# Twenty instead of sixteen seven-product pairs in the second MLP product of a hybrid decoder layer

## The chip, the cores and the metric

The kernel runs on one core of a Trainium2 chip. The metric is the time of one execution on the device in microseconds (us); less is better. The engines are named as the profile names them: PE (TensorE's matmuls) and PEld (its weight loads), DVE (VectorE), ACT (ScalarE), POOL (GpSimd) and SP (SyncE, which issues the weight loads from memory here).

## The reference

One decoder layer over 16 learned meta tokens and 256 input tokens of width 2048, in float32. Four mixers (S5, mLSTM, FoX, Pool) stand between two projections; then comes the MLP. Its last product, 256 tokens x 8192 by 8192 x 2048, is the stage that the change touches:

```python
D_MODEL = 2048
SEQ = 256
D_FF = 4 * D_MODEL
...
hn = rmsnorm(h, g_pre_ffn[l])
ff = jnp.square(jax.nn.relu(hn @ mlp_w1[l])) @ mlp_w2[l]
h = h + rmsnorm(ff, g_post_ffn[l])
```

## The kernel before

**Numbers.** Each float32 operand is split into a rounded part and the rest (high and low), and a product is three matmuls: high by high, high by low, low by high. ACT makes the high part by a cast (`wh`, line 155, and `ah`, line 201), DVE the low part by a subtraction (`wl`, line 156, and `al`, line 202). The order is fixed on each engine: DVE's subtraction waits for ACT's cast, and PE's matmuls wait for both.

**Stages.** All four projections of the layer run as one list of jobs (`stream`, line 133). A job is 1 MB of weights in two halves of 512 KB, each loaded by one transfer that SP issues (`load_job`, line 123). PE consumes half by half; the loop over halves splits weights `LOOK = 3` halves ahead into four buffers of each kind (`wsp`), and loads go three jobs ahead. The staging buffers are `wst` (8 tiles) and, apart from them, `wss` (2 tiles, one job).

**The second MLP product** (`fast_jobs`, line 286) is computed in two parts of 1024 output columns each. A part has 32 jobs, called pairs, since each covers two blocks of 128 of the 8192 inner elements. A letter in `KINDS` (line 53) says how a pair is computed:

- N, plain (`plain`, line 319): 2 inner blocks x 2 token blocks x 2 column blocks are 8 block products, three matmuls each (lines 310 to 312): 24 matmuls of 512 columns. Its weights come through `wst` and the splits at lines 155 and 156, its activations through `split_act` (line 196).
- S, seven products (`seven`, line 346): a Strassen-Winograd form with 7 block products, 21 matmuls, 9 in its first half and 12 in its second. It needs sums of weight blocks and of activation blocks ahead of its matmuls, and these are split as well. Its weights come through `wss`.

The work ahead of an S pair is a list of seven steps, taken in this order: `raw` (splits of three raw weight blocks, lines 348 and 349), `act_sums` (split of the raw activations, and four sums on POOL, lines 351 and 367), `sums1` (two differences on DVE, line 351), `act_split` (split of the activation sums), `split1` (split of two sums), `sums2` (two more differences) and `split2`. The split results stand in parts of the tile `xc`, which is free after the first MLP product. There is one copy of them, so the steps of an S pair can write a part of it only once the matmuls of the S pair before have read it; and the loads of an S pair can start only once the splits of the S pair before have read `wss`.

**The order around the change.** `stream` decides at which half i of the job list a step is recorded. `at` is the number of the S pair's first half. Steps of the first S pair begin 6 halves ahead of it, those of each later one 2 halves behind the first half of the S pair before, which is right after that pair; they are spread evenly over the halves up to 4 ahead of `at`:

```python
sums[0]["from"] = sums[0]["at"] - 6
...
left = max(1, s["at"] - 3 - i)
for _ in range(-(-len(s["steps"]) // left)):
    s["steps"].pop(0)(s["stage"])
```

Beneath, a scheduler of the tile framework turns the recorded order into one list for each engine. After the last S pair of a part its sums (in PSUM banks M1, M5, M6, M7) are combined on ACT and DVE (lines 406 to 413); the last pair (first part) or last two pairs (second part) are held and run output block by output block, and each block is then normalized, scaled and, at the end, written out.

Of the kernel before, what the change touches and what calls it, by code (L numbers as in the profile page):

```python
# [49 lines left out]
LOOK = 3  # L50
PACE = 2.0
LOOP = (2.5, 4.0, 3.0)
KINDS = ("NNNS" * 7 + "NNSN", "NNS" + "NNNS" * 6 + "NNSNN")


def build(tc, A, out):
# [10 lines left out]
class Body:  # L67
# [65 lines left out]
    def stream(self):  # L133
        nc = self.nc
        jobs = self.jobs
        sums = [j for j in jobs if "steps" in j]
        sums[0]["from"] = sums[0]["at"] - 6
        halves = [(j, h) for j in jobs for h in range(2)]
        split = {}

        def do_split(i):
            j, h = halves[i]
            if "steps" in j:
                return
            src = j["stage"][h]
            if j.get("early"):
                wh = self.sb(self.post, [P, 1024], f"wh{j['early']}{h}", F32R)
                wl = self.sb(self.post, [P, 1024], f"wl{j['early']}{h}", F32R)
            else:
                wh = self.sb(self.wsp, [P, 1024], "wh", F32R)  # L150
                wl = self.sb(self.wsp, [P, 1024], "wl", F32R)
            n = 512 if i == 0 else 1024
            for a in range(0, 1024, n):
                cs = slice(a, a + n)
                nc.scalar.copy(wh[:, cs], src[:, cs])  # L155
                nc.vector.tensor_tensor(out=wl[:, cs], in0=src[:, cs], in1=wh[:, cs].bitcast(F32), op=ALU.subtract)  # L156
            split[i] = (wh, wl)
            if j.get("pre"):
                j["pre"](h)

        done = 0
        early = [i for i, (j, h) in enumerate(halves) if j.get("early")]
        for i, (j, h) in enumerate(halves):
            self.load(i // 2 + 3)
            if i == early[0] - 2:
                self.load(early[-1] // 2 + 1)
            while done < i + LOOK + 1 and done < len(halves) and (done not in early or i >= early[0] - 2):
                with ExitStack() as es:
                    if early[-1] < done <= early[-1] + LOOK + 1:
                        for ins in self.after:  # L170
                            es.enter_context(self.tc.issue_after(ins))
                    do_split(done)
                done += 1
                if done - 1 in early:
                    while done in early:
                        do_split(done)
                        done += 1
                    break
            if sums and i >= sums[0]["from"]:
                s = sums[0]  # L180
                if "stage" not in s:
                    self.load_job(s, -1)
                left = max(1, s["at"] - 3 - i)
                for _ in range(-(-len(s["steps"]) // left)):
                    s["steps"].pop(0)(s["stage"])
                if not s["steps"]:
                    sums.pop(0)
                    if sums:
                        sums[0]["from"] = s["at"] + 2
            if i == 0:  # L190
                self.load_s5()
            self.pull(PACE + min(0.0, self.credit))
            wh, wl = split.pop(i, (None, None))
            j["mm"](h, wh, wl)
# [1134 lines left out]
    def ffn_jobs(self):  # L1329
# [82 lines left out]
        ta, tm = ["a0", "a1", "a2", "a3"], ["m0", "m1", "m2", "m3"]  # L1412
        jobs += self.fast_jobs(w2, NF, act2, 0, tm, ta, KINDS[0], 2, part_a, evac_a)
        jobs += self.fast_jobs(w2, NF, act2, 1024, ta, tm, KINDS[1], 4, part_b, evac_b)
        return jobs
# [26 lines left out]
```

## Time and profile before

| what | value |
|---|---|
| median of 3 runs | 1120.52 us (1120.06 to 1123.67) |
| the profiled execution, its own time | 1118.29 us |
| span of that execution | 1116.6 us |
| PE busy | 1092.6 us (98%), 6377 matmuls |
| DVE busy | 786.3 us (70%) |
| ACT busy | 600.6 us (54%) |
| POOL busy | 178.6 us (16%) |
| read from memory | 199.58 MB |

The profile lists, for one execution, each instruction of each engine with its start and duration. The duration of a matmul is modelled and overlaps the next one, so what a matmul takes is read from starts. In brackets behind a row stands the idle time of its engine in front of it, and what ended that. The span leaves out 1.7 us of the execution around it.

### The profile page before, as it was taken

How to read it: one execution, taken by the hardware profiler on the slowest of the kernel's cores; microseconds unless marked ns; L12 is line 12 of the kernel's file. 1: busy time of each engine (PE TensorE's matmuls, PEld its weight loads, DVE VectorE, ACT ScalarE, POOL GpSimd, SP SyncE). 2: the span in 40 equal slices, each digit the busy share in tenths (PEclk: the TensorE clock that was granted, in tenths of full speed). 3: DMA queues.
4: the chain of work that ended last, by engine and by line, in shares of the span. 5: the costliest groups of instructions: out<-in, count | busy, mean ns of one | idle time of the engine just before them, and what ended most of it. 6: DMA issues, size and time to landing. Idle time of an engine off the chain costs nothing.

```text
span 1116.6 us, 16901 instructions
## 1 busy us (share of the span) xinstructions
PE 1092.6 (98%) x6377; PEld 949.8 (85%) x6377; DVE 786.3 (70%) x1094; ACT 600.6 (54%) x919; POOL 178.6 (16%) x222
## 2 busy tenths in 40 slices
PE   8999999999999999999999999999999999999996
PEld 7899999888977878888888888888888888888885
DVE  6589997655555675555555555558788789997886
ACT  5576443356555566454445444546665555765562
POOL 7810320101342011100000000001121120421101
PEclk9899999999999999999999999999999999999998
DMA  8646555554446636666666666666546655666542
GB/s 253 194 128 191 152 151 152 159 152 127 133 154 230 233 126 218 189 188 189 188 186 188 188 186 188 187 189 227 197 172 205 223 176 187 229 194 230 197 151 76
DMA packets 94707, 203.35 MB, mean 182 GB/s; under 512 B 15877, under 2 KB 19073, under 8 KB 94369
## 3 DMA queue, kind: packets, MB, share of 16 engines
q1 hardware_dynamic: 93680, 201.46, 58.0%
q8 instruction: 50, 0.82, 0.3%
q10 hardware_dynamic: 848, 0.79, 0.2%
q14 instruction: 33, 0.26, 0.1%
q0 software_dynamic: 96, 0.02, 0.0%
HBM read 199.58 MB, written 2.11 MB: 181 GB/s over the span
## 4 chain that ended last, share of the span: by engine, by line
PE 92%; POOL 3%; DMA 2%; DVE 1%; ACT 1%; issue 1%; DVEq 0%; SPq 0%; POOLq 0%; ACTq 0%
PE m L1353 11%; PE a L1353 11%; PE a L223 6%; PE a L224 6%; PE a L225 6%; PE a L1354 6%; PE m L1354 6%; PE m L311 5%; PE m L312 5%; PE m L310 5%; PE a L311 5%; PE a L310 5%; PE a L312 5%; PE a L252 4%; PE m L252 3%; POOL row L734 1%
## 5 line engine op out<-in xcount | busy, mean ns | idle before, releaser
L156 DVE TENSOR_TENSOR wl<-wst,wh 128x1024 fp32r<-128x1024 f32 (+1 forms) x255 | 311.2, 1226 | 150.9 <-ACT wh L155 150.6
L155 ACT CAST wh<-wst 128x1024 fp32r<-128x1024 f32 (+1 forms) x255 | 265.7, 1045 | 216.6 <-PE m L1353 54.0
L1353 PE MATMUL m<-xc,wh 128*128 128x512 f32 x512 | 180.2, 394 | 0.1
L1353 PE MATMUL a<-xc,wh 128*128 128x512 f32 x512 | 179.5, 393 | 0.0
L223 PE MATMUL a<-xc,wh 128*128 128x272 f32 (+2 forms) x576 | 168.7, 295 | 0.4 <-ACT wh L155 0.4
L224 PE MATMUL a<-xc,wh 128*128 128x272 f32 (+2 forms) x576 | 167.6, 292 | 0.0
L225 PE MATMUL a<-xc,wl 128*128 128x272 f32 (+2 forms) x576 | 166.3, 291 | 0.0
L156 DVE TENSOR_TENSOR wl<-wss,wh 128x1024 fp32r<-128x1024 f32 x78 | 95.9, 1230 | 75.0 <-ACT wh L155 74.8
L1354 PE MATMUL a<-xc,wl 128*128 128x256 f32 x512 | 144.1, 282 | 0.0
L1354 PE MATMUL m<-xc,wl 128*128 128x256 f32 x512 | 144.1, 282 | 0.0
L155 ACT CAST wh<-wss 128x1024 fp32r<-128x1024 f32 x78 | 81.6, 1047 | 90.8 <-PE m L1353 29.4
L1353 PEld LDWEIGHTS m<-xc,wh 128*128 128x128 f32 x512 | 96.0, 187 | 22.3 <-DVE xc L1309 0.3
L1353 PEld LDWEIGHTS a<-xc,wh 128*128 128x128 f32 x512 | 95.9, 187 | 22.1
L223 PEld LDWEIGHTS a<-xc,wh 128*128 128x128 f32 x576 | 110.0, 192 | 4.5 <-issue 2.2
L224 PEld LDWEIGHTS a<-xc,wh 128*128 128x128 f32 x576 | 110.5, 192 | 1.0 <-issue 0.4
L225 PEld LDWEIGHTS a<-xc,wl 128*128 128x128 f32 x576 | 109.4, 191 | 0.8 <-issue 0.4
L351 POOL TENSOR_TENSOR sums<-h 128x128 f32<-128x128 f32 x12 | 20.5, 1712 | 498.3 <-DVE xc L349 468.3
L1354 PEld LDWEIGHTS a<-xc,wl 128*128 128x128 f32 x512 | 96.5, 188 | 0.1
L1354 PEld LDWEIGHTS m<-xc,wl 128*128 128x128 f32 x512 | 96.5, 189 | 0.0
L348 ACT CAST xc<-wss 128x512 fp32r<-128x512 f32 (+1 forms) x64 | 59.8, 941 | 36.4 <-DVE wss L351 28.5
L310 PE MATMUL m<-wh,ah 128*128 128x512 f32 x192 | 74.7, 389 | 0.0
L311 PE MATMUL m<-wl,ah 128*128 128x512 f32 x192 | 74.7, 389 | 0.0
(371 smaller groups left out, 1929.0 us busy)
## 6 DMA issues: line engine op xcount, KB each, us to landing
wst<-in_mlp_w SPq DMA_DIRECT2D x182, 512.0 KB, 4.2
wss<-in_mlp_w SPq DMA_DIRECT2D x74, 512.0 KB, 3.7
wst<-in_w_in SPq DMA_DIRECT2D x49, 512.0 KB, 3.9
wss<-in_w_in SPq DMA_DIRECT2D x22, 512.0 KB, 3.7
wst<-in_w_out SPq DMA_DIRECT2D x20, 512.0 KB, 3.6
wss<-in_w_out SPq DMA_DIRECT2D x12, 512.0 KB, 5.2
x<-in_x SPq DMA_DIRECT2D x8, 256.0 KB, 7.4
res<-in_x SPq DMA_DIRECT2D x1, 2048.0 KB
```

The source lines that it names most:

```text
L155: nc.scalar.copy(wh[:, cs], src[:, cs])
L156: nc.vector.tensor_tensor(out=wl[:, cs], in0=src[:, cs], in1=wh[:, cs].bitcast(F32), op=ALU.subtract)
L223: nc.tensor.matmul(acc[:, :nt], sh, xh(k, t0, nt), start=(k == 0), stop=False)
L224: nc.tensor.matmul(acc[:, :nt], sh, xl(k, t0, nt), start=False, stop=False)
L225: nc.tensor.matmul(acc[:, :nt], sl, xh(k, t0, nt), start=False, stop=(k == nk - 1))
L252: ins = nc.tensor.matmul(acc[tok, c], sp[k][a][:, tok * P:(tok + 1) * P], w2[b][:, c * 512:(c + 1) * 512], start=(k == 0 and (a, b) == (0, ...
L310: nc.tensor.matmul(b, ah, wh, start=first, stop=False)
L311: nc.tensor.matmul(b, ah, wl, start=False, stop=False)
L312: return nc.tensor.matmul(b, al, wh, start=False, stop=stop).ins
L348: nc.scalar.copy(wh, src)
L1353: nc.tensor.matmul(acc.rearrange("p (a b) -> p a b", a=2), wh[:, ws], XC[:, k, :, 0:S], start=(k == 0), stop=False)
L1354: nc.tensor.matmul(acc[:, 0:S], wl[:, ws], XC[:, k, 0, 0:S], start=False, stop=(k == NK - 1))
```

## The change

`KINDS` now has an S in every third place, ten in each part, with two N at the end: 20 S pairs and 44 N pairs instead of 16 and 48. With a period of three pairs (six halves), the steps are recorded closer together. The first S pair's begin 4 halves ahead of it instead of 6. Its loads are recorded one half before its first step. A later S pair's steps begin one half earlier than before, behind the first half of the S pair in front of it: one step there, and the other six spread up to the half that is 2 ahead of its own first.

```diff
@@ -50,7 +50,7 @@
 LOOK = 3
 PACE = 2.0
 LOOP = (2.5, 4.0, 3.0)
-KINDS = ("NNNS" * 7 + "NNSN", "NNS" + "NNNS" * 6 + "NNSNN")
+KINDS = ("NNS" * 10 + "NN", "NNS" * 10 + "NN")
 
 
 def build(tc, A, out):
@@ -134,7 +134,7 @@
         nc = self.nc
         jobs = self.jobs
         sums = [j for j in jobs if "steps" in j]
-        sums[0]["from"] = sums[0]["at"] - 6
+        sums[0]["from"] = sums[0]["at"] - 4
         halves = [(j, h) for j in jobs for h in range(2)]
         split = {}
 
@@ -176,17 +176,19 @@
                         do_split(done)
                         done += 1
                     break
-            if sums and i >= sums[0]["from"]:
+            if sums and i >= sums[0]["from"] - 1:
                 s = sums[0]
                 if "stage" not in s:
                     self.load_job(s, -1)
-                left = max(1, s["at"] - 3 - i)
-                for _ in range(-(-len(s["steps"]) // left)):
+
+                left = s["at"] - 1 - i
+                for _ in range(0 if i < s["from"] else 1 if i == s["from"] else -(-len(s["steps"]) // left)):
                     s["steps"].pop(0)(s["stage"])
                 if not s["steps"]:
+                    assert left >= 1
                     sums.pop(0)
                     if sums:
-                        sums[0]["from"] = s["at"] + 2
+                        sums[0]["from"] = s["at"] + 1
             if i == 0:
                 self.load_s5()
             self.pull(PACE + min(0.0, self.credit))
```

In the new program every line after 186 has a number 2 higher (156 stays, 202 is 204, 310 is 312, 349 is 351, 351 is 353). On TensorE's list 12 matmuls fewer stand; VectorE has 28 subtractions more.

On VectorE, in the middle of the first part, a period of the kernel before, from the last two splits of one S pair (line 349) to the first of the next (`wss` are its staging tiles; lines 156 and 202 belong to N pairs):

```order
L349 TENSOR_TENSOR xc_71<-wss_8547,xc_71 128x1024
L156 TENSOR_TENSOR wl_8579<-wst_8535,wh_8578 128x1024
L349 TENSOR_TENSOR xc_71<-wss_8548,xc_71 128x1024
L202 TENSOR_TENSOR al_8603<-h_4654,ah_8602 128x512
L156 TENSOR_TENSOR wl_8599<-wst_8536,wh_8598 128x1024
L156 TENSOR_TENSOR wl_8651<-wst_8634,wh_8650 128x1024
L202 TENSOR_TENSOR al_8675<-h_4654,ah_8674 128x512
L156 TENSOR_TENSOR wl_8671<-wst_8635,wh_8670 128x1024
L156 TENSOR_TENSOR wl_8688<-wst_8666,wh_8687 128x1024
L202 TENSOR_TENSOR al_8712<-h_4654,ah_8711 128x512
L156 TENSOR_TENSOR wl_8708<-wst_8667,wh_8707 128x1024
L349 TENSOR_TENSOR xc_71<-wss_8715,xc_71 128x512
```

The same stretch of the change:

```order
L351 TENSOR_TENSOR xc_71<-wss_8606,xc_71 128x1024
L156 TENSOR_TENSOR wl_8707<-wst_8686,wh_8706 128x1024
L351 TENSOR_TENSOR xc_71<-wss_8607,xc_71 128x1024
L204 TENSOR_TENSOR al_8731<-h_4654,ah_8730 128x512
L156 TENSOR_TENSOR wl_8727<-wst_8687,wh_8726 128x1024
L156 TENSOR_TENSOR wl_8748<-wst_8722,wh_8747 128x1024
L204 TENSOR_TENSOR al_8772<-h_4654,ah_8771 128x512
L156 TENSOR_TENSOR wl_8768<-wst_8723,wh_8767 128x1024
L351 TENSOR_TENSOR xc_71<-wss_8734,xc_71 128x512
```

Between the steps of two S pairs lie the splits of two N pairs (four of `wl`, two of `al`) where those of three lay; the steps themselves have the same order.

On SyncE, the loads of one period before:

```order
L131 DMA wss_8547<-in_mlp_w 128x1024
L131 DMA wst_8498<-in_mlp_w 128x1024
L131 DMA wss_8548<-in_mlp_w 128x1024
L131 DMA wst_8499<-in_mlp_w 128x1024
L131 DMA wst_8535<-in_mlp_w 128x1024
L131 DMA wst_8536<-in_mlp_w 128x1024
L131 DMA wst_8634<-in_mlp_w 128x1024
L131 DMA wst_8635<-in_mlp_w 128x1024
L131 DMA wss_8715<-in_mlp_w 128x1024
```

and of the change:

```order
L131 DMA wss_8478<-in_mlp_w 128x1024
L131 DMA wst_8558<-in_mlp_w 128x1024
L131 DMA wss_8479<-in_mlp_w 128x1024
L131 DMA wst_8559<-in_mlp_w 128x1024
L131 DMA wst_8594<-in_mlp_w 128x1024
L131 DMA wst_8595<-in_mlp_w 128x1024
L131 DMA wss_8606<-in_mlp_w 128x1024
```

Two loads of N pairs fewer stand between one S pair's loads and the next; one still stands between the two loads of an S pair.

## Rows read from the trace of the kernel before

**Rows 1.** The page's engine totals, and its chain of waits by engine.

```profile
PE 1092.6 (98%) x6377; PEld 949.8 (85%) x6377; DVE 786.3 (70%) x1094; ACT 600.6 (54%) x919; POOL 178.6 (16%) x222
...
PE 92%; POOL 3%; DMA 2%; DVE 1%; ACT 1%; issue 1%; DVEq 0%; SPq 0%; POOLq 0%; ACTq 0%
```

**Rows 2.** Busy time by windows: a steady stretch, and the joint of the parts.

```profile
core 0: us, PE busy (x) PEld busy (x) DVE busy (x) ACT busy (x) POOL busy (x), PEclk, DMA share, GB/s
840.00:860.00 20.00, 20.00 (x90) 16.57 (x89) 16.62 (x19) 12.51 (x15) 3.29 (x4) 1.00 0.57 196
940.00:960.00 20.00, 20.00 (x90) 16.57 (x89) 19.19 (x25) 13.93 (x22) 0.67 (x1) 1.00 0.67 215
```

**Rows 3.** Timeline of PE around an S pair (start, duration, what).

```profile
866.65 0.39 PE L310 MATMUL m<-wh,ah 128*128 128x512 f32 x1
866.88 0.39 PE L311 MATMUL m<-wl,ah 128*128 128x512 f32 x1
...
869.37 0.39 PE L310 MATMUL a<-xc,ahR 128*128 128x512 f32 x1
...
874.13 0.39 PE L310 MATMUL m<-wh,ah 128*128 128x512 f32 x1
```

**Rows 4.** Timeline of DVE through the steps of an S pair.

```profile
846.86 1.23 DVE L156 TENSOR_TENSOR wl<-wst,wh 128x1024 fp32r<-128x1024 f32 x1 [1.15 <-ACT wh L155]
848.92 0.69 DVE L202 TENSOR_TENSOR al<-h,ah 128x512 fp32r<-128x512 f32 x1 [0.84 <-ACT ah L201]
...
851.01 1.83 DVE L349 TENSOR_TENSOR xc<-wss,xc 128x512 fp32r<-128x512 f32 x2
852.76 0.68 DVE L351 TENSOR_TENSOR wss<-wss 128x512 f32<-128x512 f32 x1
...
854.56 1.82 DVE L351 TENSOR_TENSOR wss<-wss,wss 128x512 f32<-128x512 f32 x2
856.42 0.83 DVE L351 TENSOR_TENSOR wss<-wss 128x512 f32<-128x512 f32 x1
857.17 1.48 DVE L349 TENSOR_TENSOR xc<-wss,xc 128x1024 fp32r<-128x1024 f32 x1
858.58 1.21 DVE L156 TENSOR_TENSOR wl<-wst,wh 128x1024 fp32r<-128x1024 f32 x1
859.71 1.21 DVE L349 TENSOR_TENSOR xc<-wss,xc 128x1024 fp32r<-128x1024 f32 x1
860.85 0.68 DVE L202 TENSOR_TENSOR al<-h,ah 128x512 fp32r<-128x512 f32 x1
861.45 1.21 DVE L156 TENSOR_TENSOR wl<-wst,wh 128x1024 fp32r<-128x1024 f32 x1
```

**Rows 5.** Timeline of ACT: the cast that the split at 846.86 waits for.

```profile
845.77 1.05 ACT L155 CAST wh<-wst 128x1024 fp32r<-128x1024 f32 x1 [1.32 <-PE m L312]
```

**Rows 6.** Timelines of DVE and PE at the joint of the two parts.

```profile
951.09 1.22 DVE L156 TENSOR_TENSOR wl<-wst,wh 128x1024 fp32r<-128x1024 f32 x1
...
953.91 1.07 PE L311 MATMUL a<-wl,ah 128*128 128x512 f32 x4
```

**Rows 7.** Timeline of POOL: the first of its four sums of an S pair.

```profile
854.12 0.84 POOL L351 TENSOR_TENSOR sums<-h 128x128 f32<-128x128 f32 x1 [17.63 <-DVE xc L349]
```

**Rows 8.** Timelines of SP (the loads for the next S pair) and ACT (their second reader).

```profile
858.68 0.33 SPq L131 DMA_DIRECT2D wss<-in_mlp_w  x1
859.82 0.33 SPq L131 DMA_DIRECT2D wst<-in_mlp_w  x1
860.95 0.33 SPq L131 DMA_DIRECT2D wss<-in_mlp_w  x1
...
850.53 1.05 ACT L348 CAST xc<-wss 128x1024 fp32r<-128x1024 f32 x1 [0.18 <-PE m L312]
```

**Rows 9.** The page's DMA issues: count, KB each, median us to landing.

```profile
wss<-in_mlp_w SPq DMA_DIRECT2D x74, 512.0 KB, 3.7
...
wss<-in_w_out SPq DMA_DIRECT2D x12, 512.0 KB, 5.2
```

**Rows 10.** The chain that ended last: where it leaves PE.

```profile
1100.51 0.24 PE a L312
```

## Prediction

> **What bounds the kernel now.** I read the profile's engine totals and its chain of waits first. TensorE is busy for 98% of the span and carries 92% of the chain that ended last [rows 1]. So a change can gain by taking matmuls away, or lose by making TensorE wait. Next come the busy times in windows of the second MLP product. In a steady stretch TensorE has no idle time at a granted clock of 1.00 (the higher level, 2.4 GHz); VectorE is busy 16.62 of 20 us, ScalarE 12.51, GpSimd 3.29. At the joint of the product's two parts VectorE reaches 19.19, and TensorE is still full [rows 2]. So TensorE alone bounds this product, and VectorE is next in line.
>
> The rows of TensorE give the size of each kind of pair [rows 3]. The second half of a plain pair (N) starts at 866.65 and the seven-product pair (S) behind it at 869.37: 12 matmuls in 2.72 us, 0.2267 us each. The S pair ends where the next N begins, at 874.13: 21 matmuls in 4.76 us. A plain pair has 24, so it takes 5.44 us. The listed duration of 0.39 us is a modelled end; the starts, 0.2267 us apart, are what a matmul costs.
>
> **What VectorE does meanwhile** [rows 4]. Starts that follow each other without a wait give a cost of 1.13 us for a split of 1024 elements (858.58 to 859.71) and 0.60 us for one of 512 (860.85 to 861.45). An N pair asks two of the first and one of the second, 2.86 us. The steps of one S pair run from 851.01 to 860.85 with one weight split of an N pair among them: 9.84 - 1.13 = 8.71 us. A period NNNS is 3 x 5.44 + 4.76 = 21.08 us of TensorE and 3 x 2.86 + 8.71 = 17.29 us of VectorE; the other 3.79 us are waits such as the 1.15 us at 846.86 and the 0.84 us at 848.92. They end on ScalarE's casts, and the cast in front of the first of them waited 1.32 us for a matmul [rows 5]: TensorE had not yet let go of a buffer. VectorE idles because it is as far ahead as the buffers allow, so these waits are the cover, not a cost.
>
> How deep that cover is shows in one place: the split that starts at 861.45 ends at 862.66, and its first reader is the matmul at 866.88 [rows 3, 4]. Even right behind the steps of an S pair the data is 4.22 us early. At the joint it is least: a split ends at 952.31 and is read at 953.91, 1.60 us early [rows 6].
>
> **The change, part by part.** *Matmuls.* There were 16 S pairs, 8 in each part, and now there are 20. Each of the four more replaces 24 matmuls by 21, so 12 go: 12 x 0.2267 = 2.72 us. All lie on the path, since TensorE never waits in this product. The Trainium skill (page "TensorE: Matmul & The Clock Gate", section "Back-to-back issue gap") gives about 131 ns per matmul of 512 columns in a sustained stream; the rows show 226.7 ns, so the measurement decides; by the page the sum would be 1.6 us.
>
> *Steps of four more S pairs.* Each adds 8.71 us to VectorE and takes an N pair's 2.86 us away. Both parts now run in periods of NNS: 2 x 5.44 + 4.76 = 15.64 us of TensorE against 2 x 2.86 + 8.71 = 14.43 us of VectorE. The spare is 1.21 us a period where it was 3.79. It is thin but positive, so VectorE still regains its full lead before each block of steps, and the block, unchanged in content, still leaves about the 4.22 us that it leaves now. I cost it at 0. If the cover is gone, every us over 15.64 is paid in each of 20 periods. ScalarE stands at 12.51 of 20 us [rows 2], and a denser mix does not bring it near its limit: 0 as well.
>
> *GpSimd's sums.* They run directly behind the step that frees their buffer, after 17.63 us of waiting for VectorE [rows 7], so they are ready a whole period early; a period that is 5.44 us shorter leaves about 12 us. What they cost is VectorE's speed beside them: two operations from 854.56 to 856.42 instead of 1.20 us, one of 0.75 instead of 0.60, one of 1.41 instead of 1.13: 0.66 + 0.15 + 0.28 = 1.09 us, already inside the 8.71.
>
> *The loads of S pairs.* The staging buffers are freed by the last two splits of the steps; the second load is issued at 860.95 [rows 8] and lands 3.7 us later by the median [rows 9], at 864.65. Its first reader is ScalarE's cast, one period behind the one at 850.53 [rows 8], so at 871.61, 6.96 us later. With one N pair fewer, 5.44 us of that go: 1.5 us are left. That is 0 at the median, and the order in which SyncE issues the loads keeps two plain loads among and two behind these. With the slowest median landing on the page, 5.2 us [rows 9], it just fits.
>
> *Start and joint.* The first S pair is the third instead of the fourth. It has 5.44 us less, of which VectorE needed 2.86 for the N pair, so at worst 2.58 us are lost; I take 0, because in steady periods the block needs no more room than NNS gives, and 2.58 as the other bound. At the joint one more N pair now lies between the last S pair of the first part and the first of the second, so the tight spot gets easier. The end, from the last sums on, has the same instructions in the same order; it moves with TensorE.
>
> **Sum.** The profiled execution took 1118.29 us, 1116.6 of it the span. 1118.29 - 2.72 = 1115.57. The median of the runs shown is 1120.52, 2.23 above that execution, so the forecast is 1120.52 - 2.72 = **1117.8 us**, 0.24% below. About 0.3%, 3.4 us, is what a measurement of this kernel can tell from no change: this gain is real but below that.
>
> **The rivals.** *VectorE becomes the bound* (the other side). It decides once a block of steps costs over 8.71 + 1.21 = 9.92 us. The way there is GpSimd: were VectorE held for all of GpSimd's 3.29 us a block [rows 2] instead of 1.09, the block would be 10.91 us, the period 16.63, and 0.99 us x 20 periods would be lost: 1117.8 + 19.8 = 1137.6 us. For it speaks that the spare shrinks from 3.79 to 1.21 us. Against it speaks that VectorE completes operations in those us, at 0.75 to 0.93 instead of 0.60 [rows 4], and that the 19.19 of 20 us at the joint cost TensorE nothing. The Trainium skill (page "SBUF — State Buffer", section "Who interferes with whom") says that a VectorE instruction with two SBUF inputs and a GpSimd instruction that reads SBUF exclude each other, so that the second waits for the whole of the first; by that rule this rival would win, but the trace shows a slowing by about half. Chance 4%.
>
> *The S loads come late.* Landing later than 3.7 + 1.5 + 1.21 = 6.4 us stalls TensorE in each period; at 7 us it is 0.6 x 20 = 12 us: 1129.8. Nothing shown lands that late by the median; more bunched loads speak for it. Chance 4%.
>
> *A stall in one place only*, at the first S pair: up to 2.58 us back, 1120.4 us. Chance 8%.
>
> **How the numbers follow.** The forecast has 84%. That the change isn't there is no case: the order of TensorE's work has just 12 matmuls fewer. Runs of the same program spread from 1118.29 to 1123.67; both less 2.72 give the range, **1115.6 to 1121.0 us**, which also takes in the local stall. Within the forecast the step from 0.24% to 0.3% is 0.6 us, small against that spread, so I give three tenths of it to faster: 0.25. Slower by over 0.3% are the two rivals, 0.08. Within 0.3%: 0.67.
>
> **What would show it.** TensorE full in every window of this product, with starts 0.227 us apart; the matmul that now stands at 1100.51 on the chain [rows 10] at about 1097.8; VectorE near 18.5 of 20 us in steady windows (14.43 of 15.64), its waits for ScalarE mostly gone. Wrong would be: starts of TensorE over 0.3 us apart at the head of S pairs, each a period from the last, released by VectorE (first rival), or by ScalarE's cast behind a late load (second).

## The result, and the profile after

The changed kernel takes 1130.26 us (median of 6 runs, 1127.95 to 1130.98) beside 1119.28 us for the kernel before (6 runs, 1116.20 to 1123.67): a ratio of 1.0099, 95% interval 1.0083 to 1.0115. The forecast was 1117.8 us and a gain of 0.24%; it is a loss of 1%, and outside the range.

The page's engine totals and its chain of waits by engine:

```profile
PE 1095.4 (97%) x6365; PEld 947.2 (84%) x6365; DVE 804.4 (71%) x1122; ACT 603.4 (53%) x931; POOL 189.5 (17%) x238
...
PE 73%; DVE 10%; DMA 8%; issue 4%; POOL 3%; ACT 2%; SPq 0%; DVEq 0%; ACTq 0%; POOLq 0%
```

Twelve matmuls fewer (6365 instead of 6377), as worked out. But the chain that ended last, 92% TensorE in [rows 1], is now 73% TensorE, with 10% VectorE and 8% DMA: TensorE waits. Where it does is told by windows of the second MLP product (columns as in [rows 2]: busy us and instructions of each engine, TensorE's granted clock, DMA share, GB/s):

```profile
840.00:860.00 20.00, 20.00 (x90) 16.58 (x89) 17.60 (x20) 12.70 (x17) 3.30 (x4) 1.00 0.59 188
860.00:880.00 20.00, 19.55 (x87) 15.85 (x86) 16.70 (x20) 10.49 (x14) 3.30 (x4) 1.00 0.57 185
880.00:900.00 20.00, 19.39 (x85) 15.55 (x84) 16.23 (x19) 9.57 (x13) 3.30 (x4) 1.00 0.61 206
900.00:920.00 20.00, 19.14 (x83) 15.16 (x83) 16.58 (x19) 11.63 (x15) 3.29 (x4) 1.00 0.60 208
920.00:940.00 20.00, 18.93 (x82) 14.75 (x80) 17.27 (x22) 11.66 (x15) 4.43 (x6) 1.00 0.49 160
940.00:960.00 20.00, 17.42 (x62) 13.49 (x63) 20.00 (x26) 12.14 (x21) 2.22 (x3) 0.83 0.61 197
...
1020.00:1040.00 20.00, 20.00 (x90) 16.54 (x89) 17.60 (x20) 12.37 (x16) 3.30 (x4) 1.00 0.63 204
...
1080.00:1100.00 20.00, 19.49 (x86) 15.80 (x85) 17.04 (x21) 10.33 (x13) 3.29 (x4) 1.00 0.51 165
```

A full window holds 90 matmuls. The first part is full up to 860, then the windows are short of 3, 5, 7 and 8; the joint is short of 28; the second part starts full and is short again at its end. A shortage that sets in late is the mark of a lead that is eaten period by period. TensorE's first waits in this product, a period of 16.72 us apart, stand near the end of an S pair and are released by its last split:

```profile
876.61 0.50 PE L313 MATMUL a<-xc 128*128 128x512 f32 x1 [0.45 <-DVE xc L351]
...
893.33 0.50 PE L313 MATMUL a<-xc 128*128 128x512 f32 x1 [0.61 <-DVE xc L351]
```

So VectorE is late with that split, but not for its load: it is busy 16.2 to 17.3 us of 20 in the first part's short windows, below the 18.5 that the prediction expected of a full mix. (At the joint it is busy throughout, 20.00 us.) It waits. Its timeline over one period, and ScalarE's behind it:

```profile
872.80 1.48 DVE L351 TENSOR_TENSOR xc<-wss,xc 128x1024 fp32r<-128x1024 f32 x1
...
875.34 1.21 DVE L351 TENSOR_TENSOR xc<-wss,xc 128x1024 fp32r<-128x1024 f32 x1
...
881.09 0.68 DVE L351 TENSOR_TENSOR xc<-wss,xc 128x512 fp32r<-128x512 f32 x1
883.96 1.23 DVE L351 TENSOR_TENSOR xc<-wss,xc 128x1024 fp32r<-128x1024 f32 x1 [2.19 <-ACT xc L350]
...
889.52 1.48 DVE L351 TENSOR_TENSOR xc<-wss,xc 128x1024 fp32r<-128x1024 f32 x1
890.93 1.21 DVE L156 TENSOR_TENSOR wl<-wst,wh 128x1024 fp32r<-128x1024 f32 x1
892.06 1.21 DVE L351 TENSOR_TENSOR xc<-wss,xc 128x1024 fp32r<-128x1024 f32 x1
```

```profile
878.32 0.62 ACT L350 CAST xc<-wss 128x512 fp32r<-128x512 f32 x1 [0.25 <-DMA wss<-in_mlp_w]
882.87 1.05 ACT L350 CAST xc<-wss 128x1024 fp32r<-128x1024 f32 x1 [3.93 <-DMA wss<-in_mlp_w]
```

VectorE waits 2.19 us for ScalarE's cast of the raw weights, and that cast waited 3.93 us for a load. In the kernel before, this cast waited 0.18 us, and for TensorE [rows 8]. Over the whole product (767 to 1118 us) the waits of this kind sum up to (engine, line, waited for: us in total, times, longest):

```profile
ACT xc L350 <- DMA wss<-in_mlp_w: 54.8, 21, 5.0
```

The load that is late is the second of an S pair's two. SyncE's timeline of the same period:

```profile
874.31 0.33 SPq L131 DMA_DIRECT2D wss<-in_mlp_w  x1
875.45 0.33 SPq L131 DMA_DIRECT2D wst<-in_mlp_w  x1
876.58 0.33 SPq L131 DMA_DIRECT2D wss<-in_mlp_w  x1
878.32 3.20 SPq L131 DMA_DIRECT2D wst<-in_mlp_w  x3
...
893.30 0.33 SPq L131 DMA_DIRECT2D wss<-in_mlp_w  x1
```

It is issued at 876.58 and read at 882.87, 6.29 us later; the first, issued at 874.31 and read at 878.32, needs 4.0. From issue to issue of the second load it is 16.72 us, and from the split at 872.80 to that at 889.52 as well, against a TensorE period of 15.64. So the S pairs' preparation runs in a closed loop of its own: the last split of one S pair frees `wss`, the load fills it, the next S pair's steps run through their last split. The load takes 6.29 us of it, the rest 10.43. In the other steady periods of both parts the second load is read 6.1 to 7.3 us after its issue, the period is 16.5 to 17.8 us (17.0 on average over the first part's eight), and the difference of the two is 10.42 or 10.43 each time.

(The section on the kernel before gives `wst` eight tiles. It has four, one for each half of two N pairs. So an N pair's load, too, can start only once a split has freed its tile: the one issued at 875.45 follows the N split that VectorE runs from 874.21 to 875.42.)

### The profile page after: what moved, and what is told of

It reads as the page before. It is cut to its first block, busy times and chain, and to the rows that moved or that the text cites. A ratio compares the mean times of both kernels' runs of the same rounds, so it can differ in the third digit from the quotient of the medians.

```text
span 1129.2 us, 16983 instructions
## 1 busy us (share of the span) xinstructions
PE 1095.4 (97%) x6365; PEld 947.2 (84%) x6365; DVE 804.4 (71%) x1122; ACT 603.4 (53%) x931; POOL 189.5 (17%) x238
## 4 chain that ended last, share of the span: by engine, by line
PE 73%; DVE 10%; DMA 8%; issue 4%; POOL 3%; ACT 2%; SPq 0%; DVEq 0%; ACTq 0%; POOLq 0%
PE m L1355 10%; PE a L1355 10%; PE a L225 6%; PE a L226 6%; PE a L227 6%; DMA wss<-in_mlp_w 6%; PE a L1356 5%; PE m L1356 5%; PE a L254 4%; DVE xc L351 4%; DVE wss L353 3%; PE m L313 3%; PE m L312 3%; PE m L314 3%; PE m L254 2%
## 5 line engine op out<-in xcount | busy, mean ns | idle before, releaser
L156 DVE TENSOR_TENSOR wl<-wst,wh 128x1024 fp32r<-128x1024 f32 (+1 forms) x247 | 299.5, 1219 | 130.9 <-ACT wh L155 130.5
L155 ACT CAST wh<-wst 128x1024 fp32r<-128x1024 f32 (+1 forms) x247 | 256.0, 1045 | 186.0 <-PE m L1355 53.2
L350 ACT CAST xc<-wss 128x512 fp32r<-128x512 f32 (+1 forms) x80 | 75.3, 943 | 124.2 <-DMA wss<-in_mlp_w 58.1
L351 DVE TENSOR_TENSOR xc<-wss,xc 128x512 fp32r<-128x512 f32 (+1 forms) x80 | 91.2, 1142 | 40.2 <-ACT xc L350 40.2
L312 PE MATMUL a<-wh,ah 128*128 128x512 f32 x176 | 68.5, 397 | 2.4 <-ACT ah L203 1.3
```

Source lines behind the costliest of these rows:

```text
L312: nc.tensor.matmul(b, ah, wh, start=first, stop=False)
L350: nc.scalar.copy(wh, src)
L351: nc.vector.tensor_tensor(out=wl, in0=src, in1=wh.bitcast(F32), op=ALU.subtract)
```

## The experiments

Three theories. A: the closed loop, whose length is the landing of the second load plus 10.43 us. B: VectorE's amount of work is the bound, slowed by GpSimd. C: recording the steps closer together costs, not the number of S pairs. The first four kernels stand beside runs of the kernel before with a median of 1118.79 us, the last two beside others with 1118.41 us; each ratio is to these. In the cuts of edits "..." marks lines left out; each is against the changed kernel.

**e2_kinds_only**: the change's table of pairs, with the recording of the kernel before.

```diff
-        sums[0]["from"] = sums[0]["at"] - 4
+        sums[0]["from"] = sums[0]["at"] - 6
...
-            if sums and i >= sums[0]["from"] - 1:
+            if sums and i >= sums[0]["from"]:
...
-                left = s["at"] - 1 - i
+                left = max(1, s["at"] - 3 - i)
...
-                        sums[0]["from"] = s["at"] + 1
+                        sums[0]["from"] = s["at"] + 2
```

> The new table of pairs with the old recording of the steps. Theory A (a closed loop: the second load of an S pair is issued when the last split of the S pair before is done, lands 6.2 us later, and that S pair's own steps then take 10.5 us up to their last split; 16.7 us against TensorE's 15.64 a period): VectorE's and SyncE's lists in a steady period are the same as in the changed kernel, so about 1130 us, with period 16.7 us on VectorE. Theory B (VectorE's amount of work is the bound): 1130 as well. Theory C (recording the steps closer together is what costs): back to about 1117 us.

With the first S pair in third place this records its steps before the last matmuls of the first MLP product, and they overwrite a part of `xc` that those matmuls still read; so the blocks they make are of other data. The amount of work is the same, and in steady periods so is VectorE's order.

Measured: 1133.48 us, ratio 1.0125 (1.0103 to 1.0146). C falls as the cause: the old recording brings nothing back. The scheduler makes the same order in steady periods out of both, and SyncE issues the second load of an S pair every 16.2 to 17.5 us in the first part, so the loop is there with either recording. Between this ratio and the 1.0099 of the changed kernel lie about 3 us, the most that the second half of the change could be worth; no run tells whether it is.

**e3_timing_only**: the other half, the old table of pairs with the new recording.

```diff
-KINDS = ("NNS" * 10 + "NN", "NNS" * 10 + "NN")
+KINDS = ("NNNS" * 7 + "NNSN", "NNS" + "NNNS" * 6 + "NNSNN")
```

> The old table of pairs with the new recording of the steps. Theory A: a period of four pairs, 21.08 us, is longer than the loop of 16.7 us, so no loss: 1119 us, within 0.3% of the kernel before. Theory B: the same, VectorE has 3.8 us to spare a period. Theory C: slower than before by several us.

Measured: 1120.76 us beside 1118.79, ratio 1.0006 (0.9990 to 1.0021): no difference. The loss comes with the period of three pairs.

**e4_pool_queue**: GpSimd issues the S pairs' loads.

```diff
-                self.nc.sync.dma_start(dst[:, a:b], j["src"][:, a2 * h + a:a2 * h + b])
+                (self.nc.gpsimd if "steps" in j else self.nc.sync).dma_start(dst[:, a:b], j["src"][:, a2 * h + a:a2 * h + b])
```

> The changed kernel with the S pairs' loads issued by GpSimd instead of SyncE, so that N pairs' loads no longer stand between and behind them in the same queue. Theory A: if the second load lands in under 5.1 us from its issue, the loop falls under 15.64 us and TensorE is full: about 1117 us; if it still lands in 6 us or more, about 1130. Theory B: VectorE's work is untouched, 1130 us, with GpSimd's issuing perhaps adding some.

Measured: 1132.88 us, ratio 1.0123 (1.0101 to 1.0145), no gain. Its timelines of GpSimd, ScalarE and VectorE:

```profile
876.72 0.54 POOL L131 DMA_DIRECT2D wss<-in_mlp_w  x1 [1.69 <-DVE xc L351]
...
882.39 1.05 ACT L350 CAST xc<-wss 128x1024 fp32r<-128x1024 f32 x1 [2.88 <-DMA wss<-in_mlp_w]
...
872.67 1.48 DVE L351 TENSOR_TENSOR xc<-wss,xc 128x1024 fp32r<-128x1024 f32 x1
...
889.04 1.48 DVE L351 TENSOR_TENSOR xc<-wss,xc 128x1024 fp32r<-128x1024 f32 x1
```

The load issued at 876.72 is read at 882.39, 5.67 us later, and VectorE's period is 16.37 us: still over 15.64. The expectation named under 5.1 us as a gain and 6 or more as none; 5.67 lies between and is too long by A's own sum: here the rest of the loop is 16.37 - 5.67 = 10.70 us. By itself this run doesn't tell A from B. The Trainium skill (page "DMA: Bandwidth & Descriptors", section "Issuing engines are not separate DMA queues") says that loads of all issuing engines run on the same 16 DMA engines and interleave; the 0.6 us gained here are small, as that would have it. Part of this kernel's time is a loss of another kind, shown by its rows of GpSimd and ScalarE behind the joint:

```profile
960.99 11.20 POOL L353 TENSOR_TENSOR sums<-h 128x128 f32<-128x128 f32 x1 [13.88 <-DVE xc L351]
...
979.91 0.62 ACT L350 CAST xc<-wss 128x512 fp32r<-128x512 f32 x1 [10.29 <-DMA wss<-in_mlp_w]
```

The loads of an S pair stood in GpSimd's list behind this sum and were issued at 973.73 only; ScalarE waited 10.29 us for them, and the window from 980 to 1000 holds 70 matmuls instead of 90.

**e5_split2_first**: the last split goes ahead of the N split (`wl`) that stood before it.

```diff
+        self.last = {}
...
+                    for ins in self.last.pop(i, ()):
+                        es.enter_context(self.tc.issue_after(ins))
                     do_split(done)
...
-                    s["steps"].pop(0)(s["stage"])
+                    made = s["steps"].pop(0)(s["stage"])
+                    if made:
+                        self.last[i + 1] = made
...
-                hl(whT[:, 1024:2048], wlT[:, 1024:2048], st[1])
+                src, wh, wl = st[1], whT[:, 1024:2048], wlT[:, 1024:2048]
+                a = nc.scalar.copy(wh, src)
+                b = nc.vector.tensor_tensor(out=wl, in0=src, in1=wh.bitcast(F32), op=ALU.subtract)
+                return [a.ins, b.ins]
```

> The changed kernel, with the last split of an S pair's steps put ahead of the one N split that stood before it, on ScalarE and VectorE; on SyncE the two loads of an S pair then follow each other. Theory A: the loop loses the 1.13 us of that N split, and the second load lands earlier, being the second in its row and not the third: at 3.7 to 5.0 us it takes 13.1 to 14.4 us, under 15.64, so TensorE has no stall in steady periods: 1116 to 1119 us. Even with a landing of 6.2 us the loop is 15.6 us: 1119 at most. Theory B: the same work on VectorE in another order: about 1130 us.

Measured: 1116.26 us, ratio 0.9978 (0.9962 to 0.9995). Two windows, a steady one and the joint:

```profile
900.00:920.00 20.00, 20.00 (x90) 16.55 (x89) 18.91 (x21) 13.77 (x17) 3.29 (x4) 1.00 0.58 186
940.00:960.00 20.00, 20.00 (x90) 16.57 (x89) 19.55 (x24) 11.21 (x19) 4.36 (x4) 1.00 0.71 218
```

TensorE is full in both, and VectorE works more of the time than in the changed kernel (18.91 us instead of 16.58), on the same instructions. That refutes B. And in its steady periods ScalarE's cast of the second tile waits 0.17 us, for TensorE or its own cast before, and no longer for a load. But two things were moved at once, the split and, behind it, the order of the loads. The next kernel moves the loads alone.

**e7_loads_adjacent**: on SyncE, the N pair's load between the two of an S pair goes behind them.

```diff
-                self.nc.sync.dma_start(dst[:, a:b], j["src"][:, a2 * h + a:a2 * h + b])
+                with self.tc.issue_after(self.behind) if getattr(self, "behind", None) and "steps" not in j else nullcontext():
+                    ins = self.nc.sync.dma_start(dst[:, a:b], j["src"][:, a2 * h + a:a2 * h + b])
+        if "steps" in j:
+            self.behind = ins.ins
```

> The changed kernel with VectorE's and ScalarE's lists untouched; on SyncE alone the N pair's load that stood between the two loads of an S pair is put behind the second. If the slow landing (6.2 us) comes from the loads ahead of it in its row, the second load now lands in 4 to 5 us, the loop takes 14.5 to 15.5 us, under TensorE's 15.64, and the time is 1116 to 1119 us. If the slow landing comes from the loads behind it, or if the N split ahead of the last split is what counts, it stays near 6 us and 1130. Theory B (VectorE's work): 1130.

Measured: 1115.18 us beside 1118.41, ratio 0.9970 (0.9957 to 0.9984). Its SyncE timeline early in the first part (a row that merges two issues ends 0.33 us after the start of the second, which thus are at 810.54 and 826.64), and ScalarE's casts of the second tile:

```profile
808.27 2.60 SPq L132 DMA_DIRECT2D wss<-in_mlp_w  x2
...
824.37 2.60 SPq L132 DMA_DIRECT2D wss<-in_mlp_w  x2
...
839.69 2.60 SPq L132 DMA_DIRECT2D wss<-in_mlp_w  x2
```

```profile
816.22 1.05 ACT L353 CAST xc<-wss 128x1024 fp32r<-128x1024 f32 x1 [1.07 <-DMA wss<-in_mlp_w]
...
831.53 1.05 ACT L353 CAST xc<-wss 128x1024 fp32r<-128x1024 f32 x1 [0.74 <-DMA wss<-in_mlp_w]
...
846.60 1.06 ACT L353 CAST xc<-wss 128x1024 fp32r<-128x1024 f32 x1 [0.17 <-PE m L317]
```

The loop can be read off. The first of these loads is read 5.68 us after its issue, and the period is 824.37 - 808.27 = 16.10 us; the second 4.89 us, and the period is 15.32. In both cases the rest is 10.43 us, as in the changed kernel. At 4.89 us VectorE gains on TensorE, and from 846.60 on the cast waits for TensorE again, as in [rows 8]. The landing still varies: at 909.59 the cast waits 0.60 us for a load that took 5.65, and in the second part, wherever it waits for the load in a steady period, the load took between 4.4 and 6.6 us. TensorE has no gap in any window of 20 us up to 1100; its lead covers the slow ones. One load in another place gives back the whole loss.

**e9_split2_late**: the opposite dose, the last split one N half later.

```diff
+            self.lastwl = [ca.ins, cb.ins]
...
-                left = s["at"] - 1 - i
+                left = s["at"] + 1 - i
...
-                    s["steps"].pop(0)(s["stage"])
+                    with ExitStack() as es:
+                        if len(s["steps"]) == 1:
+                            for ins in self.lastwl:
+                                es.enter_context(self.tc.issue_after(ins))
+                        s["steps"].pop(0)(s["stage"])
```

> The changed kernel with the last split of an S pair's steps put one whole N half later (behind two more operations of VectorE, 0.60 + 1.13 us, so behind two N weight splits and one activation split in all); VectorE's amount of work is the same. Theory A: the loop grows by 1.73 us or somewhat more, since the second load is then the fourth in its row: a period of 18.4 us or more against 15.64. TensorE's lead of some 6.5 us is eaten in three periods of each part, and about 2.8 us are lost in each of the 15 or so others: about 1155 to 1170 us. Theory B: as the changed kernel, 1130 us.

(`ca` and `cb` are the cast and the subtraction of an N split.) Measured: 1153.18 us (4 runs, 1146.49 to 1157.63), ratio 1.0307 (1.0264 to 1.0351), a little under the span of A's expectation and far from B's. The timelines of its fastest run, of SyncE, ScalarE and VectorE:

```profile
883.44 0.33 SPq L131 DMA_DIRECT2D wss<-in_mlp_w  x1
...
888.97 1.05 ACT L355 CAST xc<-wss 128x1024 fp32r<-128x1024 f32 x1 [4.92 <-DMA wss<-in_mlp_w]
...
872.36 1.23 DVE L356 TENSOR_TENSOR xc<-wss,xc 128x1024 fp32r<-128x1024 f32 x1 [4.17 <-ACT xc L355]
...
890.05 1.23 DVE L356 TENSOR_TENSOR xc<-wss,xc 128x1024 fp32r<-128x1024 f32 x1 [3.17 <-ACT xc L355]
```

The load is read 5.53 us after its issue, and the period is 17.69 us; the rest is 12.16 us, 1.73 more than 10.43, which is what was put in. Over the first part's eight periods the mean is 18.0 us. The loop was expected at 18.4 us or more because the load, now the fourth in its row, was expected to land later still; it landed 5.2 to 6.5 us after its issue. A shorter loop than expected goes with the lower time.

## Why the prediction was wrong

**What held.** The 12 matmuls and their 2.72 us: e7 and e5, in which TensorE is full, stand 3.2 and 2.5 us below the kernel before, with intervals that hold 2.72. VectorE's work fits into the shorter period, at 18.9 us of 20 in e5. GpSimd's sums cost no more than they did: the slowed pieces of VectorE, 1.86, 0.75 and 1.41 us in [rows 4], are 1.85, 0.76 and 1.41 us in the changed kernel from 870.19 on. Of the Trainium skill's rule on the shared ports (page "SBUF — State Buffer", section "Who interferes with whom"), weighed as a rival, these runs show no more than that slowing, by a quarter to a half.

**The step that failed is the loads of S pairs**, "1.5 us are left. That is 0 at the median". The 3.7 us of [rows 9] is a median over all S-style loads of both MLP products. The one load that mattered, second of its pair and third in a row of loads that starts when a split has freed the first tile, needs 6.29 us. The changed kernel's page still gives 3.8 us for these loads, so this median could not show it, before or after. (The prediction also puts two plain loads among the S loads and two behind; by the order of the change it is one and three.) The row to look for would have been the wait of a reader. In the kernel before there is none in a steady period: the rest of the loop is already 860.95 - 850.53 = 10.42 us there [rows 8], and a period of 21.08 us leaves the load 10.66. But the last S pair of its first part has only two N pairs in front of it, and there the load, third in its row, is late:

```profile
924.19 0.33 SPq L131 DMA_DIRECT2D wss<-in_mlp_w  x1
...
930.52 1.05 ACT L348 CAST xc<-wss 128x1024 fp32r<-128x1024 f32 x1 [0.75 <-DMA wss<-in_mlp_w]
```

It is read 6.33 us after its issue. So the trace of before held the number that the forecast needed, in the one place that already had the new period.

**The second error is in the rival's threshold.** It was put at 3.7 + 1.5 + 1.21 = 6.4 us, as if VectorE's spare of 1.21 us a period could take up lateness too. It can't: while the load is late the steps stand still, they are part of the loop, and VectorE's free time before them doesn't come back. The bound is 15.64 - 10.43 = 5.2 us of landing, which is 3.7 + 1.5 without the spare; 6.29 is over it, 5.68 too (e7's first periods fell back), 4.89 is not (they caught up). So this was the second rival, priced out at 4% by a sum that counted the same slack twice. That its time of 1129.8 us is close to the measured one is chance, since it was made for a landing of 7 us against a bound of 6.4. The sign that was to tell the two rivals apart misleads as well: TensorE's waits are released by VectorE's last split, the sign of the first rival. Only two steps further back, at the cast that VectorE waits for and the load that the cast waits for, does the second show.

**What followed from it.** "VectorE still regains its full lead" fell, by 16.72 - 15.64 = 1.08 us in the period shown and 1.36 on average; TensorE ran on its lead up to its first wait, the one that ends at 876.61, and stalled in each period from then on. That "the tight spot gets easier" at the joint fell with it, for the joint needs the lead. There 28 matmuls, 28 x 0.2267 = 6.3 us, were lost; between 875 and 940 it was 23 (266 instead of the 289 that e7 has there), 5.2 us. The two are most of the 15.3 us of the profiled execution (span 1129.2 - 1116.6, and 2.72 of gain given away); the others are in the second part's end. At the joint VectorE is busy throughout (20.00 of 20 us), so that work that arrives late cannot be caught up there. In e5 and e7, which arrive with their lead, the joint is full at 19.55 and 19.59 us of VectorE, so that step was right under its condition.

**What stays open** is why a load third in its row lands 2 us later than the first. That its place counts is shown by e7; e4 and e9 show that neither the issuing queue nor the place alone sets it (5.67 and, as the fourth, 5.53 us in the periods shown).

## What to carry to other kernels

When a period gets shorter, don't only compare each engine's work with it: look for the loops that close through a buffer (last reader frees it, load, steps, last reader again), and add up the loop with the landing time of that very load, not with a median over its kind. Idle time of an engine inside such a loop is no reserve for the loop. Where a load is the loop's longest piece, its place in the issuing queue is a cheap thing to change: one load moved by one place was worth about 14 us here (11.0 lost to the kernel before without it, 3.2 won with it), and made the change the gain that it could be.

## What was not expected of the hardware

The landing of a load of 512 KB depends on its place among the others: in one period of the changed kernel 4.0 us for the first of a row and 6.29 for the third. The mean traffic of that window is only 206 GB/s, but within the row, from 875 to 883, single microseconds of the trace show 98 to 418 GB/s; whether that sets the landing, no run here shows. And at the joint, after waits of 1.30, 1.14 and 0.60 us, TensorE's matmuls came at about half speed; its timeline there, and two windows:

```profile
940.84 0.73 PE L312 MATMUL a<-wh,ah 128*128 128x512 f32 x2 [1.30 <-ACT ah L203]
942.72 0.54 PE L312 MATMUL a<-wh,ah 128*128 128x512 f32 x1 [1.14 <-DVE fm L408]
...
948.28 0.63 PE L313 MATMUL a<-wl,ah 128*128 128x512 f32 x1
948.71 0.63 PE L314 MATMUL a<-wh,al 128*128 128x512 f32 x1
```

```profile
944.00:946.00 2.00, 2.00 (x5) 1.53 (x6) 2.00 (x4) 1.05 (x1) 0.00 (x0) 0.50 0.74 244
...
950.00:952.00 2.00, 2.00 (x10) 1.64 (x9) 2.00 (x4) 1.99 (x4) 0.00 (x0) 1.00 0.78 242
```

Starts are 0.43 us apart instead of 0.227 at a granted clock of 0.50, the lower level of 1.2 GHz; from 950 on the clock is 1.00 again. From 943.85 to 949.57 that is some 13 matmuls at 0.2 us more each, an estimate of 2.7 us out of the joint's 6.3: the stalls cost more than their own length.
